# A two-layer encoder trunk on one core: small products of the state-space and delta-rule layers issued side by side, dense tap tables, norms summed from one operand

## The chip, the cores and the metric

The kernel runs on one core of a Trainium2 chip. A core has a TensorE (PE, with its weight loads shown apart as PEld), a VectorE (DVE), a ScalarE (ACT), a GpSimd (POOL), and a SyncE (SP) whose queue issues the DMAs. The metric is the device time of one execution in microseconds (us), lower is better. A profile shows one execution.

## What is computed

The input is 1024 frames of 1024 channels in fp32. Two layers follow each other; each has a token mixer and a dense MLP, and after each of the four comes a LayerNorm of `alpha * x + f(x)`.

```python
for i in range(DEPTH):                      # 2
    mix = rwkv7_time_mix(h, ...) if i == 0 else s5_mix(h, ...)
    h = layer_norm(DN_ALPHA * h + mix, ln_g[2 * i], ln_b[2 * i])
    h = layer_norm(DN_ALPHA * h + sq_relu_mlp(h, mlp_w1[i], mlp_w2[i]), ...)
```

The first mixer is a delta rule: 16 heads of 64 channels, each with a 64 x 64 state, that is decayed, corrected and read in every frame:

```python
sa = einsum('bhvk,bhk->bhv', state, a_t)
state = state * w_t + sa * b_t + v_t * k_t      # outer products
o_t = einsum('bhvk,bhk->bhv', state, r_t)
```

The second mixer (S5) is a diagonal complex state-space model: 64 groups of 16 channels, each group with 64 complex states, `s_t = abar * s_(t-1) + bbar u_t`, `y_t = Re(c s_t) + d u_t`, then GELU and a gated product with a weight of 1024 x 2048.

## The kernel before

Activations stand transposed: channels on the 128 partitions, eight tiles of 128 channels by 512 frames. The frames are two halves, A and B (`H` = 0 and 1, `HT` = 512), and the two halves are at different stages at the same time: while one is in a mixer, the dense products of the other's MLP fill PE. Dense products (`mmb`, line 188) take operands split into a high and a low part, three products each.

The program is written as tiles with a priority (`rank(base)`, lower runs first). A scheduler that models each engine's time puts the instructions of every engine in one fixed order and sets the waits; PE, DVE, ACT, POOL and SP each take their queue in that order. A pool gives a tag a number of buffers; a new tile of a tag waits until the oldest is no longer used. PSUM has four pools of banks: `pd` for dense products (3), `pl` (1), `pa` (2) and `pc` (2).

**Delta rule, chunks of 64 frames** (`core`, line 788). Eight units `m` of four chunks and eight heads follow each other. `elem` prepares decayed keys and queries; `amat` (line 580) makes the chunk matrices: 32 products of K = 64 rows by 128 columns with 128 moving elements for each unit, line 596, in four groups of eight. In a group four products belong to the head on partitions 0 to 63 and four to the head on 64 to 127; each head's four go to one `pa` bank. DVE multiplies each bank with a mask into SBUF (line 599). `invert`, `chain` and `gnorm` follow. The core stage takes about the first 1110 us; dense projections, and later the MLP of half A, fill PE meanwhile.

**LayerNorm** (`layer_norm`, line 848) is run seven times on eight tiles of a half (the eighth norm is `last_norm`, which is not touched). Two partial sums on POOL and DVE leave `a` (tiles 0 to 6) and tile 7; PE sums both over the partitions with a matrix of 1/1024 into `pm` (lines 865 and 866). Squares are added into two tiles `sa[0]` (DVE) and `sa[1]` (POOL); PE sums these for each block of 128 frames, two products a block, into `pq` (line 880).

**S5 tables** (`s5_tables`, line 1026, at about 1110 to 1275 us, beside half A's MLP) are worked out on the chip for eight tiles `f` of eight groups: `tB` (input to state), `tC` (state to output) and `tT`, the taps inside a block of `SL` = 8 frames. The taps of a tile come from PE (line 1151), are copied by ACT into a padded tile `kpad` (line 1155) whose last axis is the group, and written to DRAM by two stores (line 1159), each of which writes eight shifted copies in pieces of 512 floats.

**S5 for a half** (`s5`, line 1173; half A about 1327 to 1540 us, half B about 1859 to 2070):

1. *Turns.* The blocks of eight frames have to come to the partitions. For each pair of tiles (`f2`), 16 turns (lines 1187, 154 and 156) bring 64 blocks by 128 channels of one frame into PSUM, the lower tile by a transpose, the upper by a plain product with the identity; ACT copies them to `u1`. Then eight transposes a tile (line 1195) turn (frame, channel) to the partitions, giving `ug`.
2. *Input products* (line 1206) give the block inputs of the states, `hb`.
3. *Scan* (`advance`) over the blocks, on DVE and POOL.
4. *Output.* For each pair of tiles and each group parity `par`, the tap products (line 1250: 128 rows, 64 columns, 128 moving elements, taken from the table with a step of four floats) and the state products (line 1255: 64 rows, 64 columns, 128 moving) are added in one `pc` bank. The two tiles `j` of the pair use columns 0 to 63 and 64 to 127; `par` chooses the rows of the state products. ACT copies the bank to `y1` (line 1257), eight transposes a tile (line 1263) turn it back into a `pa` bank, DVE adds the skip (line 1265), ACT applies GELU, and a store sends it to DRAM, from where `glu` loads it.

Of the kernel before, what the change touches and what calls it, by code (L numbers as in the profile page):

```python
# [8 lines left out]
F32 = mybir.dt.float32  # L9
# [61 lines left out]
def trunk(ctx, tc, A):  # L71
# [56 lines left out]
    V.memset(cmask[:, :, 0:1], 0.0)  # L128
    mhalf = cp.tile([128, 64], F32, name="mhalf")
# [32 lines left out]
    def wload(src, kt, n, key=None):  # L162
# [19 lines left out]
        return out  # L182

# [396 lines left out]
    def amat(D):  # L580
# [7 lines left out]
        for j in range(2):  # L588
            for c2 in range(2):
                pp = [pa.tile([128, 2, 2, 128], F32, tag="a", name="pA") for h in range(2)]  # L590
                for cc in range(2):
                    for i in range(2):
                        for h in range(2):
                            hs = slice(64 * h, 64 * h + 64)
                            u = 4 * i + 2 * c2 + cc
                            PE.matmul(pp[h][:, cc, i], D.KB[j][hs, u].rearrange("p j l -> p (j l)"),
                                      D.AR[j][hs, u].rearrange("p j l -> p (j l)"), start=True, stop=True)
# [250 lines left out]
    def layer_norm(h, gi, H, split_out=True):  # L848
# [12 lines left out]
        for t in h[5:7]:  # L861
            V.tensor_add(b2, b2, t)
        V.tensor_add(a, a, b2)
        pm = plt("pm")
        PE.matmul(pm, ones_c, a, start=True, stop=False)
        PE.matmul(pm, ones_c, h[7], start=False, stop=True)
# [3 lines left out]
        for k, t in enumerate(h):  # L870
            if k < 2:
                S.activation(sa[k], t, AF.Square)
            else:
                q = lt("sq", "m")
                S.activation(q, t, AF.Square)
                (G if k % 2 else V).tensor_add(sa[k % 2], sa[k % 2], q)  # L876
        pq = plt("pq")
        for t in range(4):
            for j in range(2):
                PE.matmul(pq[:, t : t + 1], sa[j][:, t * 128 : (t + 1) * 128], ones_c[:, 0:1], start=j == 0, stop=j == 1)  # L880
# [141 lines left out]
    tT = dr.tile([KT, 128, 2, 512], F32, name="tT")  # L1022
# [3 lines left out]
    def s5_tables():  # L1026
# [78 lines left out]
        kpad = pp.tile([128, 16, 16, 4], F32, name="kpad")  # L1105
        G.memset(kpad, 0.0)
        for f in range(KT):
            gs = slice(4 * f, 4 * f + 4)
            bc = pp.tile([128, 2, 2, 4, 16], F32, tag="bc", name="bc", bufs=1)
# [43 lines left out]
            for par in range(2):  # L1153
                ps_ = slice(64 * par, 64 * par + 16)
                S.copy(kpad[ps_, 8:].rearrange("p t c g -> p g (t c)"), p[ps_])
            tv = tT[f].rearrange("(s c) two n -> two c s n", c=16)
            for par in range(2):
                src = kpad[64 * par : 64 * par + 16, 1:9].rearrange("p t c g -> p (t c g)")
                SP.dma_start(tv[par], bass.AP(src.tensor, src.offset, [src.ap[0], (64, SL), src.ap[1]]))
# [13 lines left out]
    def s5(H, h):  # L1173
# [6 lines left out]
        for f2 in range(4):  # L1180
            u1 = s5p.tile([128, 8, SL, 16], F32, tag="u1", name="u1", bufs=2)
# [214 lines left out]
```

## Time and profile before

| what | us |
|---|---|
| three runs | 2727.84, 2739.15, 2743.22 |
| median | 2739.15 |
| the profiled execution | 2746.6 |
| its span, first to last instruction | 2744.8 |

The mean granted clock of TensorE was 0.961 of full speed in the profiled execution. The profile has a page (busy shares, chain of waits, costliest groups), and the trace behind it answers questions: groups of instructions by line and shape ("x512" is the count, then busy us and the mean ns of one, then the idle time of the engine before them and what ended it), the instructions in order of time, merged into runs (start, us from the first start to the last end, engine, line, operation, shapes, count), stretches of time with the busy time of each engine, and waits. A shape such as `128*64 128x128` says 128 rows and 64 columns of the array and a moving operand of 128 partitions by 128 elements. Busy time of PE is the union of its records and says nothing of how much of the array they use.

### The profile page before, as it was taken

Reading aid. Unit: us, or ns where it says so; the run is one execution under the profiler, and the core shown is the slowest. Engines: PE = TensorE matmul, PEld = TensorE weight load, DVE = VectorE, ACT = ScalarE, POOL = GpSimd, SP = SyncE. Lnnn points to the kernel's source line nnn. Section 1 sums busy time; section 2 is a strip of 40 time slices with the busy share of each in tenths; the row PEclk is TensorE's granted clock in tenths of the full one; section 3 lists DMA queues with packets and bytes.
Section 4 is the critical chain, followed back from the end, with each engine's and each line's share of the span. In section 5 each row is a group of like instructions: output and inputs, shape, how many; then the busy total and the mean of one; then the engine's idle time right before and its main releaser. Section 6 shows DMA issues by size and latency. Waiting matters only on the chain.

```text
span 2744.8 us, 43807 instructions
## 1 busy us (share of the span) xinstructions
PE 2598.4 (95%) x16582; PEld 2089.9 (76%) x16582; DVE 1813.3 (66%) x3191; ACT 1154.8 (42%) x2038; POOL 630.6 (23%) x515
## 2 busy tenths in 40 slices
PE   7999979989899999989999999999999999999997
PEld 5778757678677777767876788778778887788886
DVE  7477677577786867997567553674855546755556
ACT  7455574544543333353532332434223324433334
POOL 3121542432442122342122000120220101210101
PEclk9989979999899999999999999999999999999998
DMA  4765455564223334545333533233343322333333
GB/s 146 235 214 175 151 164 156 178 203 142 81 86 88 93 92 148 141 129 163 100 112 127 174 95 100 81 96 112 103 164 110 96 96 81 119 96 96 96 96 100
DMA packets 215058, 345.90 MB, mean 126 GB/s; under 512 B 21184, under 2 KB 75584, under 8 KB 214848
## 3 DMA queue, kind: packets, MB, share of 16 engines
q1 hardware_dynamic: 214848, 343.10, 40.5%
q8 instruction: 131, 2.15, 0.3%
q14 instruction: 79, 0.65, 0.1%
HBM read 279.06 MB, written 63.96 MB: 125 GB/s over the span
## 4 chain that ended last, share of the span: by engine, by line
PE 44%; DVE 4%; issue 3%; DMA 1%; POOL 1%; ACT 1%; ACTq 0%; SPq 0%; DVEq 0%; POOLq 0%
PE d L188 39%; PE py L1250 1%; PE py L1255 1%; DVE wlo L149 1%; DMA wraw<-in_mw_dram 1%; PE pu L154 1%; PE pbu L1206 1%; POOL rl L975 1%; DVE hA L991 0%; DMA s_y<-yg 0%; DVE t L1218 0%; DVE hB L991 0%; ACT whi L148 0%; DVE sq L876 0%; PE pu L1195 0%
## 5 line engine op out<-in xcount | busy, mean ns | idle before, releaser
L148 ACT CAST whi<-wraw 128x512 fp32r<-128x512 f32 x668 | 413.5, 620 | 929.1 <-PE d L188 623.2
L149 DVE TENSOR_TENSOR wlo<-wraw,whi 128x512 fp32r<-128x512 f32 x668 | 500.6, 750 | 426.8 <-ACT whi L148 404.3
L188 PE MATMUL d<-qbuf,whi 128*128 128x512 f32 (+1 forms) x2112 | 657.0, 394 | 23.8 <-DVE hA L991 12.8
L188 PEld LDWEIGHTS d<-qbuf,whi 128*128 128x128 f32 x2112 | 391.8, 191 | 120.0 <-DVE hA L991 17.8
L188 PE MATMUL d<-qbuf,wlo 128*128 128x512 f32 (+1 forms) x1056 | 411.9, 392 | 10.7 <-DVE wlo L149 10.4
L975 POOL TENSOR_TENSOR rl<-rl 128x512 f32<-128x512 f32 x128 | 157.2, 1228 | 1094.5 <-ACT rl L974 1094.5
L188 PE MATMUL d<-oAh,whi 128*128 128x512 f32 (+1 forms) x960 | 390.9, 411 | 15.5 <-ACT ev L418 6.3
L188 PE MATMUL d<-oAl,whi 128*128 128x512 f32 (+1 forms) x960 | 387.5, 405 | 3.0 <-DVE oAl L149 2.8
L188 PE MATMUL d<-oAh,wlo 128*128 128x512 f32 (+1 forms) x960 | 386.5, 405 | 2.4 <-DVE wlo L149 2.3
L188 PE MATMUL d<-oBh,whi 128*128 128x512 f32 x704 | 279.2, 397 | 0.0
L188 PE MATMUL d<-oBh,wlo 128*128 128x512 f32 x704 | 278.7, 396 | 0.2 <-DVE wlo L149 0.2
L188 PE MATMUL d<-oBl,whi 128*128 128x512 f32 x704 | 277.1, 394 | 0.0
L188 PEld LDWEIGHTS d<-qbuf,wlo 128*128 128x128 f32 x1056 | 201.7, 191 | 56.5 <-DVE wlo L149 14.5
L188 PEld LDWEIGHTS d<-oAh,whi 128*128 128x128 f32 (+1 forms) x960 | 185.9, 194 | 62.2 <-ACT ev L418 8.4
L188 PEld LDWEIGHTS d<-oAh,wlo 128*128 128x128 f32 (+1 forms) x960 | 185.8, 194 | 44.4 <-DVE wlo L149 3.2
L188 PEld LDWEIGHTS d<-oAl,whi 128*128 128x128 f32 (+1 forms) x960 | 185.6, 194 | 43.1 <-DVE oAl L149 5.2
L991 DVE TENSOR_TENSOR hB<-hB,d 128x512 f32<-128x512 f32 (+1 forms) x256 | 165.0, 650 | 71.2 <-PE d L188 68.0
L991 DVE TENSOR_TENSOR hA<-hA,d 128x512 f32<-128x512 f32 x240 | 162.1, 682 | 64.4 <-PE d L188 62.1
L188 PEld LDWEIGHTS d<-oBh,wlo 128*128 128x128 f32 x704 | 132.9, 189 | 32.4 <-issue 2.0
L188 PEld LDWEIGHTS d<-oBl,whi 128*128 128x128 f32 x704 | 133.1, 189 | 29.9 <-issue 0.7
L188 PEld LDWEIGHTS d<-oBh,whi 128*128 128x128 f32 x704 | 133.1, 189 | 29.0 <-issue 1.2
L149 DVE TENSOR_TENSOR qbuf<-rl,qbuf 128x512 fp32r<-128x512 f32 x128 | 95.0, 742 | 73.5 <-ACT qbuf L148 73.5
(374 smaller groups left out, 3804.8 us busy)
## 6 DMA issues: line engine op xcount, KB each, us to landing
wraw<-in_mw_dram SPq DMA_DIRECT2D x520, 256.0 KB, 2.7
wraw<-in_glu_dram SPq DMA_DIRECT2D x64, 256.0 KB, 2.7
low<-wlo SPq DMA_DIRECT2D x52, 256.0 KB, 2.6
wlo<-low SPq DMA_DIRECT2D x52, 256.0 KB, 3.6
wraw<-in_wk_dram SPq DMA_DIRECT2D x32, 256.0 KB, 3.5
wraw<-in_wr_dram SPq DMA_DIRECT2D x32, 256.0 KB, 3.9
wraw<-in_wv_dram SPq DMA_DIRECT2D x32, 256.0 KB, 4.3
yl<-s_y SPq DMA_DIRECT2D x32, 256.0 KB, 3.1
```

Source lines behind the costliest of these rows:

```text
L148: S.copy(hi, src)
L149: (e or V).tensor_sub(lo, src, hi.bitcast(F32))
L154: PE.matmul(out, x, idt, start=True, stop=True)
L188: bulk.append((PE.matmul(p, w, x, **kw).ins, x.shape[-1]))
L975: G.tensor_mul(r, r, r)
L991: V.tensor_add(z, z, p)
L1206: PE.matmul(p[qs, g2, ri], tb[:, g2, ri, qs], u[:, 2 * g2 + par], start=True, stop=True)
L1250: PE.matmul(p[64 * j : 64 * j + 64, g2], ug[f][:, 2 * g2 + par], tv[:, par, g2], start=g2 == 0, stop=False, skip_group_check=True)
L1255: PE.matmul(p[64 * j : 64 * j + 64, g2], hb[qs, 4 * f + g2, ri, 0:NSC], tcm[qs, g2, ri], start=False, stop=ri == 1, skip_group_check=True)
```

## The change

Six edits in one:

- *Chunk matrices:* the eight products of a group are held in written order, the two heads in turn, beginning with the second head. `inorder` adds an order without a wait between neighbours (the diff defines it twice, alike).
- *Norms:* tile 7 is added on DVE, so `pm` is one product; the two sums of squares are added on DVE, so `pq` is one product a block.
- *Tap table:* its last axis is now (group, tap) and no longer (tap, group). Two pad tiles in turn; eight stores a tile, one for each parity and group, in pieces of 128 floats.
- *Block turns:* four whole transposes of 128 x 128 a tile, each of half-blocks of four frames; then two plain products for each group with a selector of the even and of the odd half-blocks, where one transpose was.
- *Output products:* both parities at once, in a `pc` and a `pa` bank; first all tap products, then the state products, held in an order that goes through both tiles and both parities, four in a row. The copies follow after both.
- *Output turns* go to the single `pl` bank.

```diff
+    sel = cp.tile([128, 2, 64], F32, name="sel")
+    V.tensor_copy(sel, ident.rearrange("p (n e) -> p e n", e=2))
...
+    def inorder(prods):
+        for x, y in zip(prods, prods[1:]):
+            tc.add_manual_dep(y.ins, x.ins.name, mybir.DependencyInfo(
+                mybir.DependencyClass.NoSync, mybir.DependencyReason.DATA), reason="order")
...
+                prods = []
                 for cc in range(2):
                     for i in range(2):
-                        for h in range(2):
+                        for h in (1, 0):
                             hs = slice(64 * h, 64 * h + 64)
                             u = 4 * i + 2 * c2 + cc
-                            PE.matmul(pp[h][:, cc, i], D.KB[j][hs, u].rearrange("p j l -> p (j l)"),
-                                      D.AR[j][hs, u].rearrange("p j l -> p (j l)"), start=True, stop=True)
+                            prods.append(PE.matmul(pp[h][:, cc, i], D.KB[j][hs, u].rearrange("p j l -> p (j l)"),
+                                                   D.AR[j][hs, u].rearrange("p j l -> p (j l)"), start=True, stop=True))
+                inorder(prods)
...
+        V.tensor_add(b2, b2, h[7])
         V.tensor_add(a, a, b2)
-        PE.matmul(pm, ones_c, a, start=True, stop=False)
-        PE.matmul(pm, ones_c, h[7], start=False, stop=True)
+        PE.matmul(pm, ones_c, a, start=True, stop=True)
...
+        V.tensor_add(sa[0], sa[0], sa[1])
         for t in range(4):
-            for j in range(2):
-                PE.matmul(pq[:, t : t + 1], sa[j][:, t * 128 : (t + 1) * 128], ones_c[:, 0:1], start=j == 0, stop=j == 1)
+            PE.matmul(pq[:, t : t + 1], sa[0][:, t * 128 : (t + 1) * 128], ones_c[:, 0:1], start=True, stop=True)
...
-    tT = dr.tile([KT, 128, 2, 512], F32, name="tT")
+    tT = dr.tile([KT, 128, 2, 4, 128], F32, name="tT")
...
-        kpad = pp.tile([128, 16, 16, 4], F32, name="kpad")
-        G.memset(kpad, 0.0)
+        kpads = [pp.tile([128, 4, 16, 16], F32, name=f"kpad{j}") for j in range(2)]
+        for kpad in kpads:
+            G.memset(kpad[:, :, 0:8], 0.0)
...
-                S.copy(kpad[ps_, 8:].rearrange("p t c g -> p g (t c)"), p[ps_])
-            tv = tT[f].rearrange("(s c) two n -> two c s n", c=16)
+                S.copy(kpad[ps_, :, 8:].rearrange("p g t c -> p g (t c)"), p[ps_])
+            tv = tT[f].rearrange("(s c) two g n -> two g c s n", c=16)
             for par in range(2):
-                src = kpad[64 * par : 64 * par + 16, 1:9].rearrange("p t c g -> p (t c g)")
-                SP.dma_start(tv[par], bass.AP(src.tensor, src.offset, [src.ap[0], (64, SL), src.ap[1]]))
+                for g2 in range(4):
+                    src = kpad[64 * par : 64 * par + 16, g2, 1:9].rearrange("p t c -> p (t c)")
+                    SP.dma_start(tv[par, g2], bass.AP(src.tensor, src.offset, [src.ap[0], (16, SL), src.ap[1]]))
...
-            for s2 in range(2):
+            for j in range(2):
                 p = pa.tile([128, 4, 128], F32, tag="a", name="pu1")
-                for j in range(2):
-                    src = h[2 * f2 + j].rearrange("p (c s) -> p c s", s=SL)
-                    for s in range(4):
-                        turn(p[64 * j : 64 * j + 64, s], src[:, :, SL - 1 - 4 * s2 - s], ident, j)
+                src = h[2 * f2 + j].rearrange("p (m s) -> p s m", s=4)
+                for s in range(4):
+                    PE.transpose(p[:, s], src[:, 3 - s], ident)
...
                 for g in range(8):
-                    PE.transpose(p[:, g], u1[ps_, g].rearrange("p s c -> p (s c)"), ident[ps_, ps_])
+                    for e in range(2):
+                        PE.matmul(p[64 * (1 - e) : 64 * (1 - e) + 64, g], u1[:, j, g].rearrange("p s c -> p (s c)"),
+                                  sel[:, e], start=True, stop=True)
...
+            pp = [r.tile([128, HT], F32, tag=t, name="py").rearrange("p (g n) -> p g n", g=4)
+                  for r, t in ((pc, "c"), (pa, "a"))]
+            for g2 in range(4):
+                for par in range(2):
+                    for j, (f, tv, tcm) in enumerate(tabs):
+                        PE.matmul(pp[par][64 * j : 64 * j + 64, g2], ug[f][:, 2 * g2 + par], tv[:, par, g2],
+                                  start=g2 == 0, stop=False, skip_group_check=True)
+            prods = []
+            for g2 in range(4):
+                for ri in range(2):
+                    for j, (f, tv, tcm) in enumerate(tabs):
+                        for par in range(2):
+                            qs = slice(64 * par, 64 * par + 64)
+                            prods.append(PE.matmul(pp[par][64 * j : 64 * j + 64, g2], hb[qs, 4 * f + g2, ri, 0:NSC],
+                                                   tcm[qs, g2, ri], start=False, stop=ri == 1, skip_group_check=True))
+            inorder(prods)
...
-                p = pa.tile([128, SL, NSC], F32, tag="a", name="pyt")
+                p = pl.tile([128, HT], F32, tag="l", name="pyt").rearrange("p (t n) -> p t n", t=SL)
```

More of the change, by code (lines that the diff above doesn't have):

```diff
@@ L182, in wload, with inorder @@
         return out
+    def inorder(prods):
+        for x, y in zip(prods, prods[1:]):
+            tc.add_manual_dep(y.ins, x.ins.name, mybir.DependencyInfo(
+                mybir.DependencyClass.NoSync, mybir.DependencyReason.DATA), reason="order")
+    def inorder(prods):
+        for x, y in zip(prods, prods[1:]):
+            tc.add_manual_dep(y.ins, x.ins.name, mybir.DependencyInfo(
+                mybir.DependencyClass.NoSync, mybir.DependencyReason.DATA), reason="order")
     bulk, hops = [], []
@@ new lines, in s5 @@
+                tabs.append((f, tt.rearrange("p two (g n) -> p two g n", g=4), tcm))
+            pp = [r.tile([128, HT], F32, tag=t, name="py").rearrange("p (g n) -> p g n", g=4)
[5 more added lines that the diff above has]
+                                  start=g2 == 0, stop=False, skip_group_check=True)
```

23 lines of the change are left out of this document (5 added, 18 removed).

## The prediction

> **What bounds the kernel now.** I read the page first (engines, chain), then the stages, then the groups by shape, then single runs in the timeline.
>
> ```profile
> span 2744.8 us, 43807 instructions
> PE 2598.4 (95%) x16582; PEld 2089.9 (76%) x16582; DVE 1813.3 (66%) x3191; ACT 1154.8 (42%) x2038; POOL 630.6 (23%) x515
> PE 44%; DVE 4%; issue 3%; DMA 1%; POOL 1%; ACT 1%; ACTq 0%; SPq 0%; DVEq 0%; POOLq 0%
> 0.00:930.00 930.00, 846.47 (x7212) 686.10 (x7213) 657.47 (x1285) 491.69 (x907) 307.06 (x259) 0.92 0.49 153
> 930.00:1110.00 180.00, 175.03 (x1135) 139.03 (x1134) 133.55 (x305) 69.39 (x127) 34.75 (x29) 1.00 0.37 114
> 1110.00:1287.00 177.00, 159.85 (x859) 122.04 (x857) 161.30 (x262) 72.14 (x111) 69.13 (x49) 0.94 0.56 151
> 1287.00:1402.00 115.00, 114.60 (x803) 93.11 (x804) 67.36 (x99) 52.20 (x90) 14.25 (x13) 1.00 0.32 102
> 1402.00:1535.00 133.00, 125.35 (x800) 94.56 (x798) 88.81 (x142) 39.00 (x66) 34.64 (x18) 0.97 0.45 149
> ```
>
> The stage rows give length, then busy us of PE, PEld, DVE, ACT, POOL, then granted clock, DMA share, GB/s. PE has work for 95% of the span. In the S5 turns (1287 to 1402) it is never free: 114.60 of 115. In the S5 scan and products (1402 to 1535) it stands 8 us of 133, in the chunk stage (0 to 930) 84 of 930, in the table stage (1110 to 1287) 17 of 177, where DVE with 161 is as full. Between the small products PE always runs dense ones of the next block, so an us taken out of PE's queue after 930 is an us of the kernel, as long as nothing it waited for gets later; before 930 it is less than that.
>
> A busy share doesn't say whether the array is well used. That is read from single runs of small products.
>
> ```profile
> L596 PE MATMUL pA<-AR,KB 64*128 64x128 f32 x512 | 65.4, 295 | 3.1 <-DVE AT L599 2.4 <-DVE kk L545 0.7
> 131.06 1.16 PE L596 MATMUL pA<-AR,KB 64*128 64x128 f32 x8
> 914.95 1.17 PE L596 MATMUL pA<-AR,KB 64*128 64x128 f32 x16
> L1250 PE MATMUL py<-tt,ug 128*64 128x128 f32 x256 | 40.4, 408 | 0.0
> 1490.55 2.01 PE L1250 MATMUL py<-tt,ug 128*64 128x128 f32 x14
> 1407.86 3.84 PE L1250 MATMUL py<-tt,ug 128*64 128x128 f32 x28
> 1328.34 2.19 PE L154 MATMUL pu<-ident,hA 128*64 128x128 f32 x16
> L1255 PE MATMUL py<-tcm,hb 64*64 64x128 f32 x512 | 32.5, 275 | 0.0
> 1492.49 1.96 PE L1255 MATMUL py<-tcm,hb 64*64 64x128 f32 x32
> 1482.90:1483.12 0.22, 0.22 (x14) 0.22 (x14) 1.00 0.13 37
> 1483.50:1483.72 0.22, 0.22 (x8) 0.22 (x6) 1.00 0.95 335
> ```
>
> A plain fp32 product leaves two records (256 chunk products, 512 records), a transpose one. A run lasts from its first start to its last end, so n records in one stream are n - 1 steps and one record's own duration. The last two rows count L1255 alone.
>
> **The change, part by part.**
>
> *Chunk matrices (L596).* Eight records of one head took 1.16 us, sixteen of both heads 1.17: heads lie on different 64 rows of the array, and issued in turn they run at once. The trace has both; the change makes every group the second kind. 32 groups of 16 at 1.17 are 37.4 us against 65.4 busy: -28.0. Each group now needs both PSUM banks before it starts, where the first head could start on one; and this is the stage in which PE has gaps. I take 70%: **-19.6**. Ends: 0 and -28.0.
>
> *Tap products (L1250).* The moving operand had a step of four floats and becomes dense. Before, the 14 records are two column streams of 8 and 6 (the tile whose table landed first had begun earlier): (2.01 - 0.41)/7 = 0.229 us a step. A product of the same 128 rows, 64 columns and 128 moving elements, but dense, is L154: 16 in one stream, (2.19 - 0.29)/15 = 0.127. So the stepped operand nearly doubles the time. With dense operands two streams of 16 should last what L1255's x32 lasts, 1.96 us; eight pairs of tiles make 15.7 against 40.4, -24.7. The x28 run has (3.84 - 0.41)/0.229 = 15 steps where two even streams would need 13, for the same reason as the x14, and such runs remain: **-22.5**. If no two streams met, 31 x 0.127 + 0.29 = 4.23 us per pair, 33.8 in all, -6.6.
>
> The Trainium skill, "SBUF — State Buffer", section "Door 1: The DMA port swizzle", speaks of 16-byte lines: each access that crosses into a new line pays. By it every element of the old operand paid and none of the new does; 0.229 against 0.127 agrees, and it would let the full -24.7 stand.
>
> *State products (L1255).* Before, two streams share the rows of one parity and differ in columns: 32 records 1.96 us. The order now goes through all four quadrants. The two windows of 0.22 us show what that gives: 8 records touch the window with two streams, 14 where the end of one parity lies over the start of the other. 64 records in four streams should thus last 1.96 us: 8 x 1.96 = 15.7 against 32.5, -16.8. The overlap in the trace is short, so **-15**; the other end is 0.
>
> *Block turns.*
>
> ```profile
> L154 PE MATMUL pu<-ident,hB 128*64 128x128 f32 x64 | 9.6, 295 | 0.0
> L154 PE MATMUL pu<-ident,hA 128*64 128x128 f32 x64 | 9.5, 294 | 0.0
> L156 PE MATMUL pu<-ident,hB 128*64 128x128 f32 x32 | 4.6, 272 | 0.0
> L156 PE MATMUL pu<-ident,hA 128*64 128x128 f32 x32 | 4.6, 272 | 0.0
> L778 PE MATMUL py<-ident,o 128*128 128x128 f32 x64 | 10.6, 287 | 0.5 <-DVE st L716 0.5
> L154 PEld LDWEIGHTS pu<-ident,hB 128*64 128x64 f32 x64 | 8.2, 209 | 1.2 <-issue 1.2
> L724 PEld LDWEIGHTS pO<-vsa,AT 128*64 128x64 f32 x512 | 19.1, 148 | 2.4
> L1195 PE MATMUL pu<-ident,u 64*128 64x64 f32 x128 | 8.1, 229 | 0.0
> L724 PE MATMUL pO<-vsa,AT 128*64 128x64 f32 x512 | 23.7, 240 | 0.0
> L1206 PE MATMUL pbu<-ug,tb 128*64 128x64 f32 x512 | 16.7, 224 | 0.0
> ```
>
> The first turns fall from 64 transposes and 64 plain products (9.6 + 9.5 + 4.6 + 4.6 = 28.3 us) to 64 transposes of 128x128. L778 is exactly that, 10.6 us, but dense; the new operand steps by four floats. The stepped weight load of L154 takes 209 ns, the dense one of L724 148, so 61 ns for 64 columns; for 128 columns that is 122 x 64 = 7.8 us at most. Between 10.6 and 18.4 I take 12.3, nearer L778, as L156, stepped too, runs no slower than L778: -16. By the line rule of the Trainium skill cited above the stepped load pays in full, which would make it -9.9. The second turns rise from 128 transposes (8.1) to 256 plain products of 128 rows into 64 columns, 512 records in two streams: L1206 puts that at 16.7, L724 in its short runs at 23.7; I take 19, **+11**. Together **-5**, ends -9.1 and +5.7. Copies out of PSUM keep number and size.
>
> *Norms.*
>
> ```profile
> L865 PE MATMUL pm<-sa,ones_c 128*128 128x512 f32 x14 | 7.1, 592 | 0.0
> L866 PE MATMUL pm<-hA,ones_c 128*128 128x512 f32 x8 | 4.2, 605 | 0.0
> L866 PE MATMUL pm<-hB,ones_c 128*128 128x512 f32 x6 | 3.2, 610 | 0.5 <-DVE hB L959 0.5
> L880 PE MATMUL pq<-ones_c,sq 128*128 128x1 f32 x112 | 16.5, 271 | 3.0 <-DVE sq L876 2.8
> L863 DVE TENSOR_TENSOR sa<-sa,sb 128x512 f32<-128x512 f32 x7 | 4.8, 687 | 0.2
> ```
>
> Half of the sums go: (7.1 + 4.2 + 3.2)/2 + 16.5/2 = 15.5 us of PE. DVE gets 14 adds of 0.687, 9.6 us, on an engine at 66%. On the norm's own path stand two adds (1.37) against one product less (about 14.5/14 = 1.04) and eight records less (8 x 16.5/112 = 1.18): no later than now. Two of seven norms lie in the stages where PE has gaps, and two adds can queue behind DVE's other work: **-10**, ends 0 and -15.5.
>
> *Table stores, banks.*
>
> ```profile
> L1159 SPq DMA_DIRECT2D tT<-kpad x16: 320/362/1264, 1128.6 to 1268.9; - x16
> SPq L169 <- DVE wlo L149: 71.4, 34, 5.6
> 1349.62 0.50 PE L188 MATMUL d<-qbuf,whi 128*128 128x512 f32 x1
> ```
>
> SP issues 64 stores for 16, in pieces a quarter as long. 48 more at 0.362 are 17 us of SP's time in a stage of 177 in which SP itself waited 71 us for DVE to free weight buffers; behind each store stand the weight loads that PE's cover needs. I take **+3**, ends 0 and +17 (0 because SP has those 71 us to spare, and the second pad buffer lets ACT write before the last store has landed). The output turns move to a single PSUM bank, so a run splits in two, and the first dense product after a small run lasts 0.50: eight more, **+2** with the wait for DVE's read; ends 0 and +8. The new selector is one DVE copy of 128 elements, once, below the 0.687 that 512 take.
>
> **Sum:** -19.6 - 22.5 - 15 - 5 - 10 + 3 + 2 = -67.1. The profiled execution took 2746.6 us (span 2744.8 and 1.8 around it), which gives 2679.5. The median of the three runs, 2739.15, lies 7.45 lower: **2672**.
>
> **Rivals.**
>
> *Evacuation takes the place of the chunk products.*
>
> ```profile
> L599 DVE TENSOR_TENSOR AT<-pA,amask 128x512 f32<-128x512 f32 x64 | 42.6, 684 | 11.8 <-PE pA L596 11.5
> 1474.00:1480.00 6.00, 4.86 (x13) 3.52 (x12) 6.00 (x8) 1.24 (x2) 3.01 (x3) 0.57 0.29 87
> ```
>
> Two reads of 0.684 follow each group, 1.37 us for 1.17 of products, from the same two banks. If groups queue behind them, the -19.6 goes: 2692. For it: DVE is the slower of the two. Against: in the 64 evacuations before, PE waited 2.4 us for them (the L596 row), and other PE work lies between groups. The Trainium skill, "TensorEngine Tiling (Array Packing)", section "PSUM Bottleneck", says the same: tiling speeds the array and not the reads from PSUM, which can then bound.
>
> *The streams don't meet.* If the order doesn't give what it says, state products stay at two streams (0) and tap products at one (-6.6): 67.1 - 15 - 15.9 = 36.2 less, 2703. Against: the 0.22 us windows and the x14 run.
>
> *Both, and SP at its dearest:* -67.1 + 19.6 + 30.9 + 14 = -2.6, 2737, no change.
>
> *Everything at its best end:* -28.0 - 24.7 - 16.8 - 9.1 - 15.5 = -94.1, 2645.
>
> *Slower: a held queue and the clock.* PE takes its work in order, so a group that waits for two banks holds the dense work behind it. The row at 1474 shows what a stand of 1.1 us does: clock 0.57 over 6 us, 2.6 us lost besides. A group that waits 1.37 and loses 2.6 costs 4 us; at 32 groups 128 us, +61, 2800. It decides from 17 of 32 groups on (67.1/4). Waits of that kind were rare before.
>
> **How the numbers follow.** Forecast 0.60 (2672, by itself 2655 to 2690); best ends 0.08 (2645); evacuation 0.11 (2692); streams 0.09 (2703); both 0.07 (2737); slower 0.05 (2800). Half a per cent, 13.7 us, is about what a measurement of this kernel can tell from no change. Faster: 0.60 + 0.08 + 0.11 + 0.09 = 0.88; same 0.07; slower 0.05. The range goes from below the best ends to above the streams case, 2640 to 2710, and leaves out 0.12.
>
> **What would show it.** L596 near 37 us busy, in runs of 16; tap products near 17; state products near 17, runs of 64 in about 2 us; transposes near 12 and second turns near 19; L880's successor at 56 records. Wrong if PE's waits for the chunk masks or for weights grow by tens of us, if the half clock gets more common before 930, or if tap products keep 0.2 us a record.

## The result, and the profile after

| kernel | median us | runs from to | profiled execution | its span |
|---|---|---|---|---|
| before | 2737.76 | 2727.84 to 2743.22 | 2746.6 | 2744.8 |
| after | 2704.24 | 2702.36 to 2707.05 | 2707.05 | 2705.3 |

Ratio 0.9883, 95% interval 0.9859 to 0.9906: 33.5 us faster, where -67 was forecast. The time lies inside the range of 2640 to 2710, but outside the 2655 to 2690 of the forecast's own case, and half of the forecast gain is missing.

First the page of the kernel after (span, engines), then its stages (length, busy us of PE, PEld, DVE, ACT, POOL, granted clock, DMA share, GB/s), then the groups that answer to those of before (busy us, mean ns of one, idle time of PE in front of them and its releaser).

```profile
span 2705.3 us, 44191 instructions
PE 2529.0 (93%) x16768; PEld 2040.5 (75%) x16768; DVE 1818.1 (67%) x3206; ACT 1147.0 (42%) x2038; POOL 626.7 (23%) x516
0.00:930.00 930.00, 831.31 (x7203) 669.78 (x7204) 648.01 (x1289) 494.07 (x910) 310.91 (x259) 0.92 0.47 153
1110.00:1287.00 177.00, 162.73 (x883) 123.21 (x883) 160.70 (x251) 67.15 (x115) 61.58 (x45) 0.97 0.55 155
1402.00:1535.00 133.00, 119.98 (x819) 94.96 (x818) 96.05 (x156) 45.53 (x79) 19.77 (x14) 0.97 0.46 157
L611 PE MATMUL pA<-AR,KB 64*128 64x128 f32 x512 | 60.0, 325 | 13.7 <-DVE AT L615 7.9 <-DVE bo L589 5.5
L1270 PE MATMUL py<-tt,ug 128*64 128x128 f32 x256 | 21.4, 279 | 7.2 <-DMA tt<-tT 7.2
L1278 PE MATMUL py<-tcm,hb 64*64 64x128 f32 x512 | 17.7, 274 | 0.0
L1206 PE MATMUL pu<-ident,hA 128*128 128x128 f32 x32 | 4.9, 281 | 0.0
L1206 PE MATMUL pu<-ident,hB 128*128 128x128 f32 x32 | 4.9, 280 | 0.0
L1213 PE MATMUL pu<-sel,u 128*64 128x64 f32 x512 | 16.7, 224 | 0.0
L1288 PE MATMUL pyt<-ident,y 64*128 64x64 f32 x128 | 11.3, 228 | 3.6 <-DVE yg L1290 3.6
L896 PE MATMUL pq<-ones_c,sq 128*128 128x1 f32 x56 | 7.5, 256 | 0.0
L882 PE MATMUL pm<-sa,ones_c 128*128 128x512 f32 x14 | 7.4, 606 | 0.5 <-DVE sa L880 0.5
```

The reader is to see two things. PE's busy time fell by 2598.4 - 2529.0 = 69.4 us, even a little more than forecast; but the span fell by 39.5 only. PE's idle time rose from 2744.8 - 2598.4 = 146 us to 176. And the idle column: chunk products (L611) and tap products (L1270) had 3.1 and 0.0 us of idle time in front of them, and now have 13.7 and 7.2.

The chunk products did not become what the forecast assumed. Two groups of the timeline of the kernel after (start, us from the first start to the last end):

```profile
212.53 0.48 PE L611 MATMUL pA<-AR,KB 64*128 64x128 f32 x2
213.24 1.16 PE L611 MATMUL pA<-AR,KB 64*128 64x128 f32 x14 [0.22 <-DVE AT L615]
219.07 0.48 PE L611 MATMUL pA<-AR,KB 64*128 64x128 f32 x2
220.16 1.16 PE L611 MATMUL pA<-AR,KB 64*128 64x128 f32 x14
```

A run of 14 records lasts as long as a whole group of 16 was to last, and two records, one product, have gone ahead by themselves for another 0.4 us.

The products of S5's output did become it. 28 dense records of the tap products last 1.96 us, where 14 took 2.01 before, and 64 records of the state products in four streams 1.98:

```profile
1463.18 1.96 PE L1270 MATMUL py<-tt,ug 128*64 128x128 f32 x28
1454.94 1.98 PE L1278 MATMUL py<-tcm,hb 64*64 64x128 f32 x64
```

The first block turns still step by four floats. Their weight loads, which overlap with products, last longer than those of the dense transposes at L794 (L778 before):

```profile
L1206 PEld LDWEIGHTS pu<-ident,hA 128*128 128x128 f32 x32 | 5.0, 206 | 0.5
L794 PEld LDWEIGHTS py<-ident,o 128*128 128x128 f32 x64 | 8.0, 147 | 3.8 <-issue 1.1 <-DVE st L732 1.0
```

The stage up to the first block turn is the same length in both kernels. Windows from the start to that turn, of the kernel before and of the kernel after:

```profile
0.00:1327.37 1327.37, 1221.31 (x9382) 979.45 (x9383) 984.25 (x1897) 652.74 (x1176) 421.01 (x345) 0.93 0.48 145
```

```profile
0.00:1325.39 1325.39, 1204.72 (x9378) 961.76 (x9379) 983.37 (x1913) 649.83 (x1183) 425.17 (x346) 0.94 0.46 146
```

PE is busy 16.6 us less there and idle 1325.39 - 1204.72 = 120.7 instead of 106.1: +14.6. What the chunk products and the first norms saved came back as idle time almost to the last us. The whole gain lies behind that point.

### The profile page after: what moved, and what is told of

It reads as the page before. It is cut to its first block, busy times and chain, and to the rows that moved or that the text cites. A ratio compares the mean times of both kernels' runs of the same rounds, so it can differ in the third digit from the quotient of the medians.

```text
span 2705.3 us, 44191 instructions
## 1 busy us (share of the span) xinstructions
PE 2529.0 (93%) x16768; PEld 2040.5 (75%) x16768; DVE 1818.1 (67%) x3206; ACT 1147.0 (42%) x2038; POOL 626.7 (23%) x516
## 4 chain that ended last, share of the span: by engine, by line
PE 63%; DVE 16%; DMA 9%; ACT 5%; issue 4%; POOL 2%; SPq 1%; ACTq 0%; DVEq 0%; POOLq 0%
PE d L202 56%; DVE wlo L151 3%; DMA s_y<-yg 1%; DMA wraw<-in_mw_dram 1%; DVE hA L1007 1%; DMA yl<-s_y 1%; DMA s_r<-ev 1%; ACT whi L150 1%; PE pA L611 1%; DVE hB L1007 1%; DVE oAl L151 1%; DVE t L1237 1%; PE pR L719 1%; PE pbu L1225 1%; PE pu L1213 1%
## 5 line engine op out<-in xcount | busy, mean ns | idle before, releaser
L202 PE MATMUL d<-qbuf,whi 128*128 128x512 f32 (+1 forms) x2112 | 658.8, 394 | 27.5 <-DVE hA L1007 14.3
L991 POOL TENSOR_TENSOR rl<-rl 128x512 f32<-128x512 f32 x128 | 147.0, 1148 | 1075.1 <-ACT rl L990 1074.9
L151 DVE TENSOR_TENSOR qbuf<-rl,qbuf 128x512 fp32r<-128x512 f32 x128 | 95.3, 745 | 65.7 <-ACT qbuf L150 65.4
```

What stands on the lines that cost most here:

```text
L151: (e or V).tensor_sub(lo, src, hi.bitcast(F32))
L202: bulk.append((PE.matmul(p, w, x, **kw).ins, x.shape[-1]))
L991: G.tensor_mul(r, r, r)
```

## The experiments

Times are medians, each set against runs of the kernel before on the same chip; the last column is (ratio - 1) x 2739 us with half its interval. By the same measure the change itself is -32 ± 6.

| run | what it is | us | ratio, interval | us to before |
|---|---|---|---|---|
| e1 | before + chunk order | 2739.70 | 1.0000 (0.9989 to 1.0011) | 0 ± 3 |
| e2 | before + norms | 2740.89 | 1.0000 (0.9988 to 1.0013) | 0 ± 3 |
| e3 | before + S5 edits | 2727.58 | 0.9955 (0.9938 to 0.9972) | -12 ± 5 |
| e5 | S5 + norms | 2711.04 | 0.9889 (0.9870 to 0.9907) | -30 ± 5 |
| e6 | S5 + chunk order | 2737.05 | 0.9991 (0.9980 to 1.0003) | -2 ± 3 |
| e11 | S5 + half of the norms' edit | 2709.73 | 0.9893 (0.9878 to 0.9908) | -29 ± 4 |
| e4 | after, whole chunk groups | 2703.71 | 0.9867 (0.9849 to 0.9885) | -36 ± 5 |
| e7 | after, five table buffers | 2701.59 | 0.9867 (0.9843 to 0.9891) | -36 ± 7 |
| e12 | e7 once more | 2705.70 | 0.9871 (0.9848 to 0.9894) | -35 ± 6 |
| e8 | after, chunk products twice | 2744.08 | 1.0009 (0.9996 to 1.0021) | +2 ± 3 |
| e9 | after, 192 early dense records fewer | 2699.84 | 0.9854 (0.9836 to 0.9873) | -40 ± 5 |
| e10 | after, 192 early dense records more | 2750.83 | 1.0045 (1.0029 to 1.0061) | +12 ± 4 |
| e13 | after, 192 late dense records fewer | 2670.82 | 0.9745 (0.9720 to 0.9771) | -70 ± 7 |
| e14 | before + norms' records, no adds | 2731.49 | 0.9971 (0.9958 to 0.9984) | -8 ± 4 |
| e15 | e4 and e7 together | 2694.63 | 0.9842 (0.9819 to 0.9866) | -43 ± 6 |

**The parts alone.** e1, e2 and e3 each take one part of the diff; nothing else is edited.

> The kernel before with the order of the chunk products alone (heads in turn, fixed order); norms and S5 as before. Theory (order alone does not make whole groups: each bank is allotted at its first use, so one product goes alone and seven follow): 0 to -6 us against before; chunk products stay at 58 to 62 us of busy time, and PE's gaps before 930 us grow by 10 to 15 us. Rival (the order is worth its 20 us and the other edits' new waits ate it): -15 to -22 us, gaps before 930 us as before (about 76 us).

> The kernel before with the norms' edit alone (one operand for the sum over channels and for the sum of squares); all else as before. Theory (PE's records are halved, 14 to 16 us of busy time go, and the stages after 930 us hand most of it on): -8 to -14 us. Rival (the added vector sums stand on the path of a norm, whose statistics PE then waits for): -4 us to +6 us, with the records halved all the same.

> The changed kernel with the chunk products' order and the norms' sums as before: the S5 edits alone (four state products in a row, tap table dense and in eight stores, block turns, one bank for pyt). Theory (the busy time goes as forecast, but a third of it comes back as PE's gaps in S5's output stage): -20 to -30 us against before, the gaps behind the tap products' table loads and the turns back of the output (some 12 us more than before) present. Rival (these gaps are not of S5's own making but come with the plan that the chunk order shifts): -38 to -45 us, those gaps as in the kernel before.

The chunk order alone gives nothing: the theory's side, and its upper end. The window up to the first turn and the group, of the kernel with the chunk order alone:

```profile
0.00:1331.18 1331.18, 1206.40 (x9388) 965.24 (x9389) 981.53 (x1900) 653.78 (x1179) 426.96 (x345) 0.93 0.47 145
L603 PE MATMUL pA<-AR,KB 64*128 64x128 f32 x512 | 59.4, 324 | 9.5 <-DVE AT L607 6.3 <-DVE bo L581 2.7 <-DVE kk L551 0.4
```

PE is 14.9 us less busy than before over that stage and 124.8 - 106.1 = 18.7 us more idle. The norms alone give nothing either: the rival's side. S5 alone gives 12, less than either theory gave it. So the singles sum to 12 where the change has 32: the parts don't add up, which no theory had.

**Whole chunk groups.** In front of the products of a group both banks are written, so that the group owns both before it starts:

```diff
                 prods = []
+                held = [V.memset(t[:, 0, 0, 0:1], 0.0) for t in pp]
...
+                tc.add_manual_dep(held[1].ins, held[0].ins.name, mybir.DependencyInfo(
+                    mybir.DependencyClass.NoSync, mybir.DependencyReason.DATA), reason="banks")
                 inorder(prods)
```

> The changed kernel, in which both banks of a group of chunk products are first written by a small vector memset (one column of each; 64 memsets), so that no product starts before the group has both banks. Theory (the lone first product costs the gain): 26 of 32 groups go as 16 records in a row at about 1.2 us, chunk products 40 to 45 us of busy time against 60, and the time falls by 8 to 15 us against the changed kernel (-41 to -48 against before). Rival (before 930 us what leaves PE's queue is not time of the kernel, since a stream of vector and scalar work sets the stage): busy time falls the same, PE's gaps before 930 us grow by as much, and the time stays within 4 us of the changed kernel or rises.

Timeline, group and start of this kernel:

```profile
220.33 1.16 PE L612 MATMUL pA<-AR,KB 64*128 64x128 f32 x16
L612 PE MATMUL pA<-AR,KB 64*128 64x128 f32 x512 | 45.6, 315 | 19.4 <-DVE pA L606 19.4
0.00:1324.69 1324.69, 1192.66 (x9378) 956.45 (x9379) 990.65 (x1977) 651.17 (x1183) 419.48 (x346) 0.93 0.47 146
```

Now most groups are whole, 16 records in 1.16 us, and the products take 45.6 us: 19.8 less than before, of the 28.0 that the forecast saw going and as much as the 19.6 that it counted on. It buys nothing. Idle time before them is 19.4 us, since PE now stands until both banks are free, and the start lasts 1324.69 against 1325.39. The broken groups were real, but mending them gives the time back as waits for the banks; the rival of this run holds.

**What an us of PE is worth, early and late.** Three runs price PE's queue by dense work on which no recurrence hangs, one by the chunk products. e9 and e13 drop as many records in two places, e9 in the key and receptance projections, e13 in the two products of S5's output gate:

```diff
-            dense(p, w, xm)
+            for k in range(KT):
+                if k < 5:
+                    mm3(p, w[k][0], w[k][1], xm[k][0], xm[k][1], k == 0, False)
+                else:
+                    mmb(p, w[k][0], xm[k][0], start=False, stop=k == KT - 1)
...
```

(A second place, where two products share a loop, gets the same.) e10 puts `mmb(p, w[0][0], xm[0][0], start=True, stop=True)` six times in front of `dense(p, w, xm)`, and the like in the second place, and e8 writes `for cc in (0, 0, 1, 1)` in the chunk products.

> The changed kernel with every chunk product issued twice in a row: 256 more products, some 50 to 65 us more PE busy time, all before 930 us. It prices PE's queue there. Theory (PE's gaps before 930 us, 90 us in all, are waits for ScalarE's and vector's work, and work added beside them is part swallowed): the time rises by 20 to 40 us against the changed kernel, and the gaps before the last chunk product shrink. Rival (an us of PE's queue is an us of the kernel there, as forecast): it rises by 50 to 65 us, with the gaps unchanged.

> The changed kernel without six of the 24 records of each key and receptance projection (the two products with a low part, for the last three of eight blocks; what they add is left out): 192 dense records fewer, all before 930 us, 43.5 us of PE at 0.227 us a record, in no place that a recurrence waits for. It prices PE's queue there from below. Theory (the start has PE gaps of 120 us and a limit beside PE, so what leaves the queue comes back as gaps): the time falls by 5 to 25 us against the changed kernel and the gaps up to the first block turns grow by 18 us or more. Rival (PE's queue does set it, and the chunk order failed by its own waits for banks alone): it falls by 35 to 45 us, the gaps as they were.

> The changed kernel with six dense records more ahead of each key and receptance projection (one product repeated, then overwritten): 192 records more, 43.5 us of PE before 930 us. It prices the queue there from above. Theory (a limit beside PE near the present length): the time rises by less than the work added, 10 to 35 us, the gaps shrinking. Rival (PE's queue sets it): 40 to 48 us, the gaps as they were.

> The changed kernel without six of the 24 records of each of the 32 products of S5's output gate (the two products with a low part, for the last three of eight blocks; what they add is left out): the same 192 dense records, 43.5 us of PE, as in the run that dropped them before 930 us, but after S5, where PE is busy 97% of the time or more. Theory (the queue is the path there, as forecast): the time falls by 36 to 45 us against the changed kernel (-68 to -78 against before). Rival (the vector engine's sums and ScalarE's parts set the pace there too): it falls by less than 30 us, PE's gaps after 1535 us growing by 12 us or more.

The windows up to the first turn, of the kernel with 192 records fewer there and of the one with 192 more:

```profile
0.00:1318.39 1318.39, 1182.19 (x9187) 943.11 (x9188) 989.64 (x1912) 648.46 (x1182) 418.69 (x346) 0.92 0.47 147
```

```profile
0.00:1366.94 1366.94, 1242.52 (x9571) 1000.91 (x9572) 998.47 (x1912) 650.48 (x1182) 421.54 (x346) 0.94 0.46 141
```

With 43.5 us of work less, PE is only 22.5 us less busy (in the run that was profiled its small products took 12 us longer, 319.7 for 307.5, and the clock was 0.92), and its idle time rises from 120.7 to 136.2; the start shortens by 7 us. With 43.5 us more it lengthens by 41.6. Against the change's -32 the medians say -8 ± 8 and +44 ± 8. So the time of e9 is what its theory said, and that of e10 what its rival said.

In e9 the missing gain is not all idle time, though. The rows have its granted clock at 0.92, where the kernel after had 0.94. By the clock records of the two traces the start of e9 has 215 us at half clock (a granted clock of 0.5) and that of the kernel after 167, and 22 us more of PE's busy time went into it. So 7 us of gain, 15.5 of idle time and 22 of clock make up the 43.5 to within 1 us. The clock is not an accident of the one execution: it is 0.952 to 0.958 in all four runs of e9 and 0.962 to 0.966 in the four of the change. Why it is lower, no run shows. In e10 (0.961 to 0.964) and in e4 (0.960 to 0.967) it is close to that of the change, so there it explains nothing.

The chunk products twice cost 34 ± 7 for 88.0 - 60.0 = 28 us of busy time (not the 50 to 65 expected, as long runs are cheap), the same answer. Late, in the output gates behind S5, the same 43.5 us are worth 70 - 32 = 38 ± 9: there the forecast's premise holds, if not quite in full.

A start in which added work costs all of itself and removed work returns next to nothing is what two paths of about equal length would give, PE's queue and one through the other engines. That is a reading; which instructions make up the second path no run has shown. For e9 the lower clock is the larger part; what stands at an equal clock is e1 and e4, where the chunk products' busy time came back as idle time.

**Why the parts don't add up.** e5 and e6 leave out one part of the change, e11 takes S5 and the norms' sum over channels (`pm`) alone.

> The changed kernel with the chunk products issued as before: S5 edits and norms' sums together. Alone these two gave -12 and +1 us, the whole change -33. Theory (the chunk order is worth nothing in any company; S5 and norms together make the 33): -28 to -35 us against before. Rival (the singles add up, and the chunk order is what releases the rest): -8 to -15 us.

> The changed kernel with the norms' sums as before: S5 edits and chunk order together. Theory (it is the norms' edit that turns S5's 12 us into 33, since before it PE waits 8 to 9 us in each S5 stage for the residual sums of the vector engine, and after it 3): -10 to -16 us against before, and in the S5 stages PE's waits for the sums hA and hB of the second MLP product at 7 us or more each. Rival (the norms add nothing; the chunk order does): -28 to -35 us, with those waits near 3 us.

> The changed kernel with the chunk order and the norms' sums of squares as before, so S5's edits and the norms' sum over channels alone. This has half of the norms' saving (some 7 us of PE), and in PE's queue the same dense work stands between S5's products as with both edits (139 and 375 records in the first stage, where S5 alone has 162 and 390). Theory (the norms' edit is worth what it is by where it puts S5 in the queue, not by the records that it saves): -24 to -31 us against before, S5's stages at 180 to 184 us each with 11 to 13 us of gaps. Rival (by its records): -16 to -22 us, the stages at 195 us with 16 us of gaps or more.

The chunk order is nothing in this company too (-30 without it, -32 with it). Without the norms S5's gain shrinks to -12, or to -2 with the chunk order, which costs 10 ± 6 there. Not quite half of the norms' saving, 7 of 16 us of PE, brings all of it, which speaks for the theory of e11. Windows of the two S5 stages, first block turn to last output turn, of the kernel before, of S5 alone, of S5 with one sum, and of the kernel after:

```profile
1327.40:1533.90 206.50, 198.85 (x1418) 154.44 (x1416) 123.11 (x193) 71.65 (x122) 38.81 (x22) 0.98 0.41 134
...
1858.60:2062.70 204.10, 196.74 (x1412) 153.49 (x1410) 122.30 (x191) 69.94 (x121) 37.55 (x22) 0.98 0.39 128
```

```profile
1323.70:1520.50 196.80, 178.90 (x1545) 143.75 (x1543) 128.42 (x191) 70.14 (x121) 38.82 (x21) 0.98 0.44 142
...
1848.10:2046.50 198.40, 181.86 (x1546) 146.15 (x1545) 126.21 (x190) 68.97 (x120) 35.10 (x22) 0.97 0.42 132
```

```profile
1327.40:1509.40 182.00, 171.04 (x1508) 137.62 (x1507) 120.89 (x183) 66.47 (x114) 33.96 (x21) 0.97 0.48 152
...
1841.60:2021.50 179.90, 169.04 (x1507) 136.38 (x1506) 120.44 (x181) 65.06 (x113) 33.78 (x21) 0.98 0.42 140
```

```profile
1325.40:1506.80 181.40, 169.80 (x1508) 136.60 (x1506) 120.10 (x181) 66.18 (x113) 33.47 (x21) 0.98 0.44 151
...
1841.10:2024.00 182.90, 170.65 (x1501) 137.01 (x1499) 118.77 (x179) 64.15 (x112) 33.10 (x21) 0.96 0.41 139
```

Length less PE's busy time is its idle time: before 7.6 and 7.4 us, S5 alone 17.9 and 16.5, S5 with one sum 11.0 and 10.9, after 11.6 and 12.2. By the groups S5's own products take (40.4 + 32.5 + 28.3 + 8.1 + 16.7 + 8.1)/2 = 67 us a stage before and (21.4 + 17.7 + 9.8 + 16.7 + 16.7 + 11.3)/2 = 47 after (16.7 is `pbu`, the same in both); so each stage gains 20 and gives back 10 if S5 is alone, 4 in the other two. Much of the other shortening is dense work that moved out of the stage (before, S5 alone and after: 554, 553 and 516 records in the first one). The two sums of the norm don't touch S5; what differs in these stages is where S5's products stand in PE's queue among the dense work. What PE waits for in the first stage, in S5 alone and in the kernel after (us, times, longest):

```profile
PE d L202 <- DVE hB L1005: 7.7, 4, 4.4
PE py L1268 <- DMA tt<-tT: 6.0, 2, 3.4
```

```profile
PE pyt L1288 <- DVE yg L1290: 3.4, 3, 1.5
PE d L202 <- DVE hB L1007: 3.1, 5, 1.2
...
PE py L1270 <- DMA tt<-tT: 1.7, 2, 0.9
```

Of the 20 us between S5 alone and the whole change, 34.4 - 23.8 = 10.6 are idle time of these two stages. Over the whole run, however, that idle time is not gone. In the profiled executions PE stands 2725.6 - 2562.3 = 163.3 us in S5 alone and 2706.5 - 2539.6 = 166.9 in e5, S5 with the norms, whose span is 19.1 us shorter: it is the busy time that fell there, by 22.7 us. The records of the seven norms are 15 of these (`pm` and `pq` together 29.9 and 14.8).

The granted clock differs as well. It is 0.957 to 0.964 (mean 0.959) in the eight runs of S5 alone and 0.956 to 0.961 (0.958) in the twelve of e6, but 0.961 to 0.968 (0.963) in the five of e11 and 0.962 to 0.966 (0.964) in the four of the change. 0.004 of 2700 us are 11 us of full clock. So of what the company seems to be worth, up to about half may be clock; that is an estimate, as no run held the clock fixed. Nor did a run change the planned order alone, so the scatter that a new plan brings by itself is not known.

**Taking S5's new waits away.** `amask` and `pick` move to the pool that ends before S5, and output rows go into the buffers of the turned blocks, which makes room:

```diff
...
-                tt = s5p.tile([128, 2, 512], F32, tag="tab", name="tt", bufs=4)
+                tt = s5p.tile([128, 2, 512], F32, tag="tab", name="tt", bufs=5)
...
-                y = s5p.tile([128, HT], F32, tag="yg", name="yg", bufs=1)
+                y = s5p.tile([128, HT], F32, tag="ug", name="yg", bufs=8)
```

> The changed kernel with a fifth buffer for S5's tables, and S5's output rows in the buffers of the turned blocks (eight in place of one). Theory (PE's queue stands at the tap products until a table lands, and at the turns back until the one output row is stored): PE's waits for the tap table (1.7 and 5.5 us in the two stages) and for pyt's bank (3.4 and 0.2 us) go to under 2 us together, and the time falls by 5 to 10 us against the changed kernel. Rival (the vector engine's and ScalarE's work of the output sets these stages, so another wait takes their place): the named waits go, others grow, and the time stays within 4 us of the changed kernel.

> The kernel with five table buffers once more, beside the others on this chip. Theory (S5's two stages are 8 us better for it in the profile, and the start, whose code is the same, was disturbed by 16 us in the run profiled): 5 to 9 us below the changed kernel's -33 against before, with the start's length back at 1325 to 1333 us. Rival (the fifth buffer, or amask and pick in another place, costs the start what S5 gains): within 3 us of the changed kernel, the start at 1338 us or more.

(e12 is the same kernel as e7, with the new chunk order.) The waits of the first S5 stage in e12:

```profile
PE d L202 <- DVE hB L1007: 9.6, 4, 4.5
...
PE pyt L1288 <- ACT y L1282: 1.2, 1, 1.2
```

In this stage the waits for the table and for `yg` are gone (in the second, 1.1 and 2.4 us are left; the change has 10.8 in both stages), and the dense products now wait 9.6 us for DVE's residual sums where they waited 3.1: the rival of e7. Both runs lie 3 to 4 us below the change, within the scatter. The start's 1341.7 us in e7's profile was 1330.6 in e12's, so that was no cost of the edit.

**The norms' records without the adds.** As e2, without the two lines that add on DVE, so the sums lack a block and half of the squares.

> The kernel before with the norms' records halved and no vector sum added: the sum over channels leaves out the eighth block, the sum of squares its second half. Theory (the added vector sums, in the path from the last residual to the norm and ahead of PE's evacuations on the vector engine, ate the records' gain): -8 to -14 us against before, where the norms' edit alone was 0, and PE's waits for the residual sums stay near the 14 us of before, not the 29 us of the norms' edit. Rival (the records are hidden in waits that PE has in a norm anyway): -4 to +3 us, PE's gaps growing by what the records save.

Windows between the two S5 stages, of the kernel before and of e14:

```profile
1533.90:1858.60 324.70, 323.15 (x1423) 263.07 (x1424) 192.70 (x287) 119.42 (x204) 47.80 (x43) 1.00 0.32 97
```

```profile
1520.10:1844.60 324.50, 320.38 (x1403) 263.10 (x1404) 192.53 (x288) 120.28 (x204) 47.00 (x43) 0.99 0.32 97
```

Both theories hold in part. The adds cost 8 ± 5 us: -8 without them, 0 with them. But the stretch, which holds two norms, is as long as before: PE is 2.8 us less busy in it and idle 4.1 us instead of 1.6. What PE's dense products wait for on the residual sums after 930, in the kernel before, in e2 and in e14:

```profile
PE d L188 <- DVE hA L991: 9.9, 14, 1.4
...
PE d L188 <- DVE hB L991: 4.4, 8, 1.1
```

```profile
PE d L188 <- DVE hA L991: 18.0, 15, 3.7
PE d L188 <- DVE hB L991: 10.8, 10, 2.3
```

```profile
PE d L188 <- DVE hA L989: 12.6, 11, 4.3
PE d L188 <- DVE hB L989: 8.9, 8, 4.1
```

14.3 us before, 28.8 with the norms' edit, 21.5 without its adds: the adds are half of that rise. Without them PE's idle time over the whole run is 2730.0 - 2575.9 = 154.1 us, 7.7 more than before, and these waits are 7.2 of it.

**A version that is faster still.** e15 holds the chunk groups' banks and has the five buffers.

> The changed kernel with both banks of a chunk group held before its first product, and with five table buffers and eight output rows in S5. Theory (the first gives the start nothing, the second gives S5 8 us of which the rest returns part): -35 to -40 us against before, within 7 us of the changed kernel. Rival (the whole chunk groups and the shorter S5 stages add up): -45 us or better.

-43 ± 6, between the two expectations and 11 ± 9 us better than the change; the two intervals (0.9819 to 0.9866, and 0.9859 to 0.9906) overlap a little. Its median of 2694.63 is the lowest of a kernel that computes all of the output.

## Why the prediction was right in direction and short by half

The step that failed is the price of what leaves PE's queue early: 70% of 28.0 us for the chunk products, -19.6, of which nothing came that can be told from 0. The second is the -10 for the norms, and with it the assumption that the parts add up. The busy time of S5's own products was forecast well.

- **Tap products:** -19.0 us of busy time (40.4 to 21.4) for -22.5. The dense operand does what was said; 7.2 us of waiting for the table, which weren't there before, take back a third.
- **State products:** -14.8 for -15. The four streams meet, 64 records in 1.98 us.
- **Block turns:** 28.3 to 9.8 and 8.1 to 16.7, together -9.9 for -5. The second turns cost what the L1206 row of before had, and not the 19 I took; the 64 stepped transposes took 9.8 us where the 64 dense ones of L778 had 10.6, so the stepped operand cost no busy time of PE. It shows in their weight loads alone, 206 ns against 147 of the dense ones, and these 59 ns are not the 122 that I reckoned for 128 columns. (The transposes of L156, which stepped too, had 133 ns a load before, so no plain price of a step comes out.) The Trainium skill, "SBUF — State Buffer", section "Door 1: The DMA port swizzle", has each access that crosses into a new 16-byte line pay; the tap products agree (40.4 to 21.4), these transposes only in their weight loads.
- **Output turns in one bank:** +3.2 busy and 3.6 of waiting for +2. **Stores:** no loss shows; PE's idle time from 1110 to 1287 was 17.1 us and is 14.3 (162.73 busy of 177 in the stages of after).
- **S5 together** was to give -37.5 (-22.5 - 15 - 5 + 3 + 2). In busy time its products gave what was said, -19.0 - 14.8 - 9.9 + 3.2 = -40.5, as the single errors cancel. As time it gives -12 alone; with the norms, for which -47.5 was forecast, -30.
- **Chunk matrices:** 0 for -19.6. This step failed. It was "I take 70%" of 28.0 us, of a stage about which the same text said that an us of the queue is worth less there. In the kernel after only 5.4 us of busy time went (65.4 to 60.0), since the groups broke up, and the wait in front of these products grew by 10.6 (3.1 to 13.7). In e1 6.0 went and the wait grew by 6.4 (to 9.5); in e4 19.8 went and it grew by 16.3 (to 19.4). So PE stood in front of the chunk products for most of what they gave up, or for more. Nearly all of these waits are for DVE: in the kernel after 7.9 us for the masked copies (L615) and 5.5 for `bo` (L589), which is read out of a `pa` bank too, in e4 all 19.4 for the writes that take the banks. This is the mechanism of the rival of 2692, evacuation, which had the loss right, its -19.6 gone. It is not proved to be the limit: no run gave the groups a third bank, and where another path sets the pace PE's idle time has to stand somewhere.
- **Norms:** 0 alone for -10. The records went as counted, 16 us; the adds on DVE cost 8 of them, the rest came back as idle time, most of it dense products that wait for residual sums. The step was the choice of 10 by share of the stages; "no later than now" counted only the norm's own path and left out who else waits for DVE.
- **The premise** that an us of PE's queue after 930 is an us of the kernel: nearly, in the gates behind S5 (38 ± 9 of 43.5), and within S5, where 4 to 10 of 20 us came back as idle time, for half or more. The border at 930 was not right: up to the first block turn, near 1325, the profiles differ by 2 us. Between 930 and 1325 no run prices the queue by itself.
- **The clock** was a term only of the slower rival. Between kernels of this record the granted clock differs by up to 0.009 (e9 and the change), 24 us of full clock, as much as the single terms of the sum.
- **The slower rival** needed 17 groups of 32 that wait; nine waits of 19.4 us came at most, in e4. Its price rests on the row at 1474 as the work of a stand of 1.1 us; the trace has one of 2.25 us shortly before, from 1471.2 to 1473.5, so the row doesn't show what 1.1 us alone do. The time of 2704 is that of "the streams don't meet", 2703, by chance: the streams met.

So 0 instead of -19.6 for the chunk order, and -30 instead of -47.5 for S5 and the norms together, make -30 for -67.1, against the -32 measured. How the -30 divides between S5 and the norms stays open, as do the clock's share in it and the path that holds the start.

## What to carry to other kernels

Before you price what leaves a queue, ask of each stage what added and what removed work costs there: a pair of kernels with some dense records more and fewer tells whether the queue is the bound, and it may be the bound upwards only. Compare the granted clock of such a pair before you read it: here it took half of what the smaller kernel saved. An average share of busy time, 95% here, does not show any of this. Where a schedule is planned as a whole, try an edit in the company in which it will live, since the same S5 edits were worth 12 us alone, 2 with the chunk order, and 30 with a norms' edit that by itself gave 0.

## Not expected of the hardware

Chunk products of both heads in a long run get cheap: 512 records more added 28 us, 0.055 us a record, against 60.0/512 = 0.117 in the broken groups. A product issued by itself between dense ones costs 0.42 us of PE, as much as six records within a run (runs of 8 take 0.64 to the start of what follows, of 14 1.08). And the granted clock stood at 0.55 for the 3.9 us behind a wait of 6.4 us of PE:

```profile
378.00:386.00 8.00, 5.99 (x63) 1.00 0.95 290
386.00:393.10 7.10, 0.78 (x6) 0.52 0.99 312
393.10:397.00 3.90, 3.86 (x11) 0.55 0.18 54
397.00:402.00 5.00, 2.65 (x42) 1.00 0.00 2
```

These are windows of the kernel after with PE's busy time alone; the dense records behind the wait go at 0.43 us each instead of 0.23.
